# Routers on the plain activations, norms by a diagonal product, adaptive units moved between products

## The chip, the cores and the metric

The kernel runs on one core of a Trainium2 chip. The metric is the device time of one execution in microseconds; three executions of the kernel before took 1907.48, 1910.18 and 1911.77 us (median 1910.18). A profiled execution of it took 1905.38 us; its trace spans 1903.6 us. All rows below are of that execution.

## The reference, cut to what matters

`x` is 256 tokens of 1024 numbers. Two blocks follow each other; every layer has a norm in front and adds its output to `x`.

- First block: `x += token_mixer(rmsnorm(x, norm_mix))`, then `x += hierarchical_moe(rmsnorm(x, norm_ffn))` with 32 experts of width 512, of which each token takes two.
- Second block, layer 0: `x += g_m * attention(modulate(x, g, sh_m, sc_m))` (its keys also come from a context), then `x += g_f * ec_moe(modulate(x, g, sh_f, sc_f))` with 16 experts of width 1024, each of which takes its 32 best tokens. Layer 1: the same with a short convolution in place of the attention.

```python
def rmsnorm(x, g):
    return x * lax.rsqrt(jnp.mean(x * x, axis=-1, keepdims=True) + EPS) * g
def modulate(x, g, shift, scale):
    return rmsnorm(x, g) * (1 + scale) + shift
# sh_m, sc_m, g_m, sh_f, sc_f, g_f of a layer:
m = jax.nn.silu(cond) @ w_ada + b_ada          # 1024 x 6144, split in six
# router of the second block's experts:
aff = jax.nn.softmax(h @ w_router, axis=-1)    # h = modulate(x, ...)
```

The weights of all experts and projections are float32 and are read from HBM once, about 713 MB in all.

## The kernel before, in words

**Stages.** `build` (L1452) runs five stages one after the other: `mixer1` (L599), `moe1` (L977), `mixer2` (L1165, attention), `moe2(0)` (L1384), `mixer3` (L1330, convolution), `moe2(1)`. `x` lies in SBUF as [128, 2, 1024]: 128 tokens on the partitions, two halves `c`. After `moe1` stands a branch for overfull experts (`moe1_overflow`, L1050); no instruction is moved across it.

**The weight stream.** `Stream` (L170) issues all weight loads on SyncE's queue, in the order that `plan` (L395) lists them, each of 2 MB into a slot of a ring. The ring has 6 slots; three more ("rooms" X, Y, Z) are lent while no mixer needs them. A load is issued once the slot of its tile is free, that is once the last reader of the tile before has run; `done` is called in program order behind it. So the stream runs ahead of the compute by up to 9 slots and then stands.

**Norms.** `norm_T` (L275) makes the normed and transposed activations. For each `c`: ScalarE squares `x` in two halves with a running sum, VectorE adds the two sums and EPS, GpSimd takes the power -0.5 (`rstd`, L264), VectorE and ScalarE write `x * rstd` into `xh`, TensorE transposes it in eight 128x128 pieces into PSUM, and `evac_mod` applies gain and shift, piece by piece, in turn on ScalarE and VectorE. In a mixer the result is then split into a high and a low fp32r part (`split`, L309).

**Products of the mixers.** `staged` (L314) splits a 128x512 piece of the weights on ScalarE (`wh`) and VectorE (`wl`), three buffers deep; `three` (L323) runs the three fp32r products (high by high, low by high, high by low). `chain` (L154) runs the projections one after the other: product, then the rest of what follows the product before it (`finish`: head norms, rope, transposes). A projection holds two of the four PSUM banks `pj`. `flow` (L143) runs the heads of the attention as overlapping units.

**Adaptive units.** `ada_unit` (L530) makes one of the six vectors of a layer: 2 x 8 float32 matmuls of [128 x 32] by [128 x 512] on two weight tiles, an evacuation each, 8 transposes, a small reduction. (0,0), (0,1), (0,2) run inside the two flows of `mixer1`, (0,3) at its end (L844), (0,4) in front of the norm of `mixer2` (L1180), (0,5) and (1,0) among its heads, (1,1) and (1,2) at its end (L1326), (1,3) and (1,4) between the halves of `mixer3`, (1,5) at its end (L1380).

**Routers.** `moe1` and `moe2` norm and transpose `x` (`norm_T`, L983 and L1391), multiply by the router's weights (`router`, L847) and then find each expert's tokens on VectorE, with short products on TensorE between. `experts` (L875) gathers the tokens of four experts at a time from `xh` (L890, `xg_ps`), multiplies by gate and up (L904, `gu_ps`), after which the slots of these weights are free, transposes, multiplies by down (L931) and scatters into four PSUM banks `y` (L943). `add_out` (L972) adds them to `x`.

**Order.** The order on SyncE is the program's; on the other engines a planner orders the instructions by its own estimate of when their operands are there, in program order where two are ready.

Of the kernel before, what the change touches and what calls it, by code (L numbers as in the profile page):

```python
# [10 lines left out]
F32 = mybir.dt.float32  # L11
# [36 lines left out]
def small_inputs(I):  # L48
# [105 lines left out]
def chain(units):  # L154


    last = iter(())
    for product, finish in units:
        next(product, None)
        for _ in last:  # L160
            pass
        for _ in product:
            pass
        next(finish, None)
        last = finish
    for _ in last:
        pass

# [59 lines left out]
class Net:  # L228
    def __init__(self, ctx, tc, I, packs, out):
        self.packs = packs  # L230
        self.ctx, self.tc, self.nc, self.I, self.out = ctx, tc, tc.nc, I, out
        self.flip = 0

# [41 lines left out]
    def norm_T(self, src, xh, dst, G, SH, ps, tag, bufs, chunks=(0, 1)):  # L275


        nc = self.nc
        for c in chunks:
            ss = self.sm.tile([128, 2], F32, tag="nh_ss", name="nh_ss")  # L280
            x, t = src(c), xh(c).rearrange("p k m -> p (k m)")
            for h in range(2):
                nc.scalar.activation(t[:, h * 512:h * 512 + 512], x[:, h * 512:h * 512 + 512], AF.Square,
                                     scale=1.0 / 32, accum_out=ss[:, h:h + 1])
            r = self.rstd(ss[:, 0:1], [128, 1], ss[:, 1:2])
            v = x.rearrange("p (m k) -> p k m", k=8)
            for h in range(2):
                i, o = v[:, 4 * h:4 * h + 4, :], xh(c)[:, 4 * h:4 * h + 4, :]
                if h == 0:
                    nc.vector.tensor_scalar(o, i, r, None, op0=ALU.mult)  # L290
                else:
                    nc.scalar.activation(o, i, AF.Copy, scale=r)
            for kq in range(2):
                b = ps.tile([128, 4, 128], F32, tag=tag, name="xT_ps", bufs=bufs)
                for kk in range(4):
                    nc.tensor.transpose(b[:, kk, :], xh(c)[:, 4 * kq + kk, :], self.ident)
                if isinstance(dst, tuple):
                    for kk in range(4):
                        k = 4 * kq + kk
                        self.evac_mod(b[:, kk, :], b[:, kk, :], G[:, k:k + 1], None if SH is None else SH[:, k:k + 1])  # L300
# [3 lines left out]
                for kk in range(4):  # L304
                    k = 4 * kq + kk
                    self.evac_mod(dst(k)[:, c * 128:c * 128 + 128], b[:, kk, :], G[:, k:k + 1],
                                  None if SH is None else SH[:, k:k + 1])

    def split(self, hi, lo, src):  # L309

        self.nc.scalar.activation(hi, src, AF.Copy)  # L311
        self.nc.vector.tensor_tensor(lo, src, hi.bitcast(F32), op=ALU.subtract)  # L312

    def staged(self, src, wk):  # L314
# [5 lines left out]
        self.split(v[0], v[1], src)  # L320
# [55 lines left out]
    def rope_tables(self, rt, wk, cos, sin, gains, parts):  # L376
# [4 lines left out]
        for qk in range(2):  # L381
# [13 lines left out]
    def plan(self):  # L395
        I, add = self.I, self.st.add

        def ada(l, v):
            src = I["ada_w_2"][l].rearrange("(p k) f -> p k f", k=8)
            for hf in range(2):  # L400
# [33 lines left out]
        for c0 in (768, 0):  # L434
# [1064 lines left out]
```

## Time and profile before

| | us |
|---|---|
| median of three executions (lowest, highest) | 1910.18 (1907.48, 1911.77) |
| profiled execution | 1905.38 |
| span of its trace | 1903.6 |
| TensorE matmuls busy | 1327.5 (70%) |
| VectorE busy | 502.8 (26%) |
| ScalarE busy | 382.2 (20%) |
| GpSimd busy | 97.4 (5%) |

The profile's page cuts the span in 40 slices of 47.6 us and gives for each the bytes that the DMA engines moved. Its line GB/s reads about 430 in the slices of the experts, and between 127 and 373 in the first five, in the 15th to 19th and in the 28th to 31st, which are the mixers. Times of the trace count from the start of the span. "PE" is TensorE, "PEld" its weight loads, "DVE" VectorE, "ACT" ScalarE, "POOL" GpSimd, "SP" SyncE. A float32 matmul of the program shows as two instructions, a transpose as one.

### The profile page before, as it was taken

The page shows a single profiled execution, that of the slowest core. Times are in us where ns is not written, and L with a number is a line of the kernel's source. Part 1 is how long each engine was busy: PE and PEld are TensorE (multiplying, and loading weights), DVE is VectorE, ACT ScalarE, POOL GpSimd, SP SyncE. Part 2 cuts the span into 40 slices and gives each one's busy share as a digit, 9 for nine tenths or more (in the row PEclk, how much of TensorE's full clock was granted, in tenths as well). Part 3 has the DMA queues.
Part 4 walks back from the last instruction along what each step waited for, and adds up shares of the span by engine and source line. Part 5 has one row for each costly group of instructions (what it writes and reads, how often), then busy time and mean ns, then how long its engine had stood idle before and what let it go on. Part 6 is the DMA issues. An engine that isn't in the chain of part 4 may idle for free.

```text
span 1903.6 us, 27293 instructions
## 1 busy us (share of the span) xinstructions
PE 1327.5 (70%) x11779; PEld 734.0 (39%) x11779; DVE 502.8 (26%) x1256; ACT 382.2 (20%) x838; POOL 97.4 (5%) x151
## 2 busy tenths in 40 slices
PE   6989776676788678997656555565996664654744
PEld 4666443343444356463222221223983221211311
DVE  4566311121111056563010010103664110101101
ACT  6545100120101054651000000003443000000000
POOL 2120000000000024110000000000000000000000
PEclk9989988898999899898887787778997877877878
DMA  9746899999999994378999999999957999999998
GB/s 373 282 156 250 358 429 429 429 427 425 401 415 430 424 355 159 127 317 339 431 431 429 431 430 431 431 430 416 346 229 307 430 430 432 430 430 430 431 430 338
DMA packets 97690, 716.14 MB, mean 376 GB/s; under 512 B 5664, under 2 KB 7840, under 8 KB 56480
## 3 DMA queue, kind: packets, MB, share of 16 engines
q1 hardware_dynamic: 97104, 712.80, 89.8%
q8 instruction: 93, 1.52, 0.3%
q0 software_dynamic: 464, 1.57, 0.2%
q14 instruction: 29, 0.24, 0.0%
HBM read 713.30 MB, written 1.05 MB: 375 GB/s over the span
## 4 chain that ended last, share of the span: by engine, by line
DMA 44%; PE 24%; DVE 3%; ACT 2%; POOL 2%; issue 1%; SPq 0%; POOLq 0%; DVEq 0%; ACTq 0%
DMA w<-in_moe_w_up 17%; DMA w<-in_moe_w_gate 12%; DMA w<-in_moe_w_down 9%; PE gu_ps L904 7%; PE cv_ps L328 4%; DMA w<-in_w_up 3%; PE pj_ps L328 2%; DMA w<-in_conv_w_in 2%; PE cx_ps L1140 2%; PE d_ps L931 2%; PE ada_ps L540 1%; PE o_ps L328 1%; PE xg_ps L890 1%; DMA w<-in_attn_w_in 1%; POOL rs_r L272 1%
## 5 line engine op out<-in xcount | busy, mean ns | idle before, releaser
L904 PE MATMUL gu_ps<-w,xgT 128*32 128x256 f32 (+1 forms) x4096 | 434.9, 584 | 312.0 <-DMA w<-in_moe_w_up 258.5
L904 PEld LDWEIGHTS gu_ps<-w,xgT 128*32 128x32 f32 x4096 | 147.5, 129 | 576.0 <-issue 259.2
L910 DVE TENSOR_TENSOR h<-gu_ps,hs 64x256 f32<-64x256 f32 (+1 forms) x64 | 46.6, 728 | 783.1 <-ACT hs L909 783.1
L909 ACT ACTIVATE hs<-gu_ps 64x256 f32<-64x256 f32 (+1 forms) x64 | 31.2, 488 | 923.9 <-PE gu_ps L904 923.9
L931 PE MATMUL d_ps<-w,eh 128*32 128x256 f32 x3072 | 201.4, 410 | 21.7 <-DMA w<-in_moe_w_down 9.4
L311 ACT ACTIVATE wh<-w 128x512 fp32r<-128x512 f32 x184 | 115.1, 631 | 130.0 <-PE pj_ps L328 44.0
L312 DVE TENSOR_TENSOR wl<-w,wh 128x512 fp32r<-128x512 f32 x184 | 125.2, 689 | 60.5 <-ACT wh L311 57.1
L931 PEld LDWEIGHTS d_ps<-w,eh 128*32 128x32 f32 x3072 | 96.2, 117 | 103.8 <-issue 25.2
L328 PE MATMUL pj_ps<-wh,roomX 128*128 128x512 f32 x352 | 102.1, 404 | 6.7 <-DVE xn L355 3.4
L923 PE MATMUL t_ps<-kp,h 64*128 64x64 f32 x192 | 25.2, 238 | 88.6 <-DVE h L910 85.6
L272 POOL TENSOR_TENSOR rs_r<-rs_r,mhalf 128x1 f32<-128x1 f32 (+3 forms) x48 | 49.7, 1035 | 588.1 <-DVE rs_r L269 327.9
L328 PEld LDWEIGHTS pj_ps<-wh,roomX 128*128 128x128 f32 x352 | 65.8, 191 | 25.4 <-issue 7.1
L890 PE MATMUL xg_ps<-Sg,xh 128*128 128x128 f32 x512 | 70.6, 297 | 4.1 <-DVE Sg L883 3.5
L328 PE MATMUL cv_ps<-roomX,wh 128*128 128x256 f32 x384 | 70.2, 284 | 1.8 <-ACT roomX L311 1.5
L890 PEld LDWEIGHTS xg_ps<-Sg,xh 128*128 128x128 f32 x512 | 65.2, 207 | 14.2 <-issue 8.8
L328 PE MATMUL pj_ps<-wl,roomX 128*128 128x512 f32 x176 | 58.3, 407 | 13.2 <-DVE wl L312 13.2
L923 PEld LDWEIGHTS t_ps<-kp,h 64*128 64x128 f32 x192 | 16.6, 137 | 128.6 <-DVE h L910 114.1
L328 PEld LDWEIGHTS cv_ps<-roomX,wh 128*128 128x128 f32 x384 | 60.1, 192 | 3.9 <-ACT roomX L311 2.6
L328 PE MATMUL cv_ps<-roomX,wl 128*128 128x256 f32 x192 | 54.2, 283 | 0.0
L540 PE MATMUL ada_ps<-w,sc 128*32 128x512 f32 x384 | 48.1, 617 | 2.8 <-DVEq L1057 2.8
L943 PE MATMUL z<-ysb,WT 32*128 32x256 f32 x512 | 36.7, 400 | 16.5 <-DVE ysb L938 16.5
L1140 PE MATMUL cx_ps<-w,roomX 128*128 128x512 f32 x96 | 43.6, 602 | 0.0
(366 smaller groups left out, 1315.7 us busy)
## 6 DMA issues: line engine op xcount, KB each, us to landing
w<-in_moe_w_gate SPq DMA_DIRECT2D x64, 2048.0 KB, 38.7
w<-in_moe_w_up SPq DMA_DIRECT2D x64, 2048.0 KB, 29.0
w<-in_moe_w_down SPq DMA_DIRECT2D x63, 2048.0 KB, 33.0
w<-in_w_gate SPq DMA_DIRECT2D x32, 2048.0 KB, 20.1
w<-in_w_up SPq DMA_DIRECT2D x32, 2048.0 KB, 23.2
w<-in_w_down SPq DMA_DIRECT2D x32, 2048.0 KB, 22.0
w<-in_ada_w SPq DMA_DIRECT2D x24, 2048.0 KB, 12.2
w<-in_attn_w_in SPq DMA_DIRECT2D x7, 2048.0 KB, 14.3
```

Source lines behind the costliest of these rows:

```text
L272: nc.gpsimd.tensor_tensor(r, r, self.mhalf.to_broadcast(shape), op=ALU.pow)
L311: self.nc.scalar.activation(hi, src, AF.Copy)
L312: self.nc.vector.tensor_tensor(lo, src, hi.bitcast(F32), op=ALU.subtract)
L328: self.nc.tensor.matmul(o, l[a], r[b], start=first and n == 0, stop=last and n == 2)
L540: nc.tensor.matmul(b[32 * j:32 * j + 32, :], self.sc[:, 4 * kk + j, :], w[:, 4 * kk + j, :], start=kk == 0, stop=kk == 1)
L890: nc.tensor.matmul(b[:, k, :], self.xh[:, c, 2 * kq + k, :], Sg[:, c].rearrange("p e s -> p (e s)"), start=c == 0, stop=c == 1)
L904: nc.tensor.matmul(gu[32 * j:32 * j + 32, :], xgT[:, k, sl:sl + 32], w[:, n * Fh:n * Fh + Fh], start=k == 0, stop=k == 7)
L910: nc.vector.tensor_tensor(h, gu[0:64, :].rearrange("p (m c) -> p c m", c=nch), hs.rearrange("p (m c) -> p c m", c=nch), op=ALU.mult)
L923: nc.tensor.transpose(ht[:, c * 64:c * 64 + 64], h[:, c, :], self.ident[0:64, 0:64])
L931: nc.tensor.matmul(d[32 * j:32 * j + 32, :], hT[:, c, n * 32:n * 32 + 32], wd(n, c, j), start=i == 0, stop=i == 2 * nch - 1)
L943: nc.tensor.matmul(y[j][:, c, :], WT[r, c * 128:c * 128 + 128], ysb[r, :], start=e == 0 and c == 0, stop=e == ne - 1, skip_group_check=True)
L1140: nc.tensor.matmul(b, xr["hT"][:, k, c * 128:c * 128 + 128], w[:, k, :], start=k == 0, stop=k == 7)
```

## The change

- The norm of a mixer no longer writes `x * rstd`. ScalarE squares `x` in one piece, GpSimd adds EPS and takes the power, VectorE writes `diag(rstd)`, and TensorE multiplies the eight pieces of `x` by it, which transposes and scales at once. In `mixer1` the gain moves into the staging of the weights.
- `held` keeps an instruction in program order on its engine. It is put on the squares, on the first four stagings behind a norm, and on a few small ones.
- The routers' norm: the mixers' last additions to `x` are followed by squares on ScalarE (`squares`), the routers transpose `x` itself (`raw_T`), the gain is multiplied into the router's weights beforehand, the shift becomes a bias of the logits (`router_bias`), and `rstd` scales the logits. The gather reads `x` with `rstd` in the selection matrix `Sg`. The residual `x` is added into the PSUM banks by eight products with the identity at expert 3, and `new_x` copies the banks out.
- Adaptive units: (0,0) and (0,1) go between the first three products of `mixer1`, (0,2) between the two of its second chain, (0,3) into the router of `moe1`, (0,4) behind the norm of `mixer2`, (1,0) and (1,1) between its five products, (1,2) among its heads, (0,5) and (1,5) into the routers of `moe2`. The order of their loads follows. The rows of the gate of `mixer3` are made at expert 2 of `moe2(0)`.
- The silu of the conditions and its data come first in `mixer1`; the forget gate comes behind two steps of the first product.

```diff
-def chain(units):
+def chain(units, fill=iter(()), last=iter(())):
...
         next(finish, None)
+        next(fill, None)
         last = finish
...
     def rstd(self, ms, shape, more=None):
-        if more is None:
-            nc.vector.tensor_scalar(r, ms, EPS, None, op0=ALU.add)
...
+            nc.gpsimd.tensor_tensor(r, ms, more, op=ALU.add)
+        nc.gpsimd.tensor_scalar(r, ms, EPS, None, op0=ALU.add)
         nc.gpsimd.tensor_tensor(r, r, self.mhalf.to_broadcast(shape), op=ALU.pow)
...
+            self.held(nc.scalar.activation(junk(c), x, AF.Square, scale=1.0 / 32, accum_out=ss))
+            r = self.rstd(ss, [128, 1])
+            nc.vector.tensor_scalar(self.diag[:, c, :], self.ident, r, None, op0=ALU.mult)
...
-                    nc.tensor.transpose(b[:, kk, :], xh(c)[:, 4 * kq + kk, :], self.ident)
+                    nc.tensor.matmul(b[:, kk, :], v[:, 4 * kq + kk, :], dg, start=True, stop=True)
...
+    def staged(self, src, wk, g=None):
...
+        if self.late:
+            self.late -= 1
+            for ins in both:
+                self.held(ins)
...
     def add_gated(self, b, gate, c, hf):
...
+        self.squares(b, c, hf)
+    def squares(self, b, c, hf):
+        self.nc.scalar.activation(b, self.x[:, c, hf * 512:hf * 512 + 512], AF.Square, scale=1.0 / 32,
+                                  accum_out=self.ss[:, hf, c:c + 1])
...
+    def raw_T(self, hT, ps):
+        v = self.x.rearrange("p c (m k) -> p c k m", k=8)
+        for kq in range(2):
+            for c in range(2):
+                b = ps.tile([128, 4, 128], F32, tag="a", name="xT_ps", bufs=3)
+                for kk in range(4):
+                    self.nc.tensor.transpose(b[:, kk, :], v[:, c, 4 * kq + kk, :], self.ident)
+                self.evac(hT[kq][:, :, c * 128:c * 128 + 128], b, c == 0)
...
             self.evac(r, b, True)
             self.st.done(("ada", l, v, hf))
-        for _ in range(1 + wait):
+            yield
+        for _ in range(wait):
             yield
...
+    def experts(self, ne, F, posm, comb, rk, G, SH, tiles, wk, ps, y, hook=None, gate=None, first=None):
...
+                nc.vector.tensor_tensor(Sg, Sg, rk[:, :, None, None].to_broadcast([128, 2, 4, 32]), op=ALU.mult)
...
-                            nc.tensor.matmul(b[:, k, :], self.xh[:, c, 2 * kq + k, :],
+                            nc.tensor.matmul(b[:, k, :], xv[:, c, 2 * kq + k, :],
...
+            if e == 0:
+                first()
...
+            if e == 3:
+                for c in range(2):
+                    for j in range(4):
+                        nc.tensor.matmul(y[j][:, c, :], self.ident, self.x[:, c, 256 * j:256 * j + 256], start=False,
+                                         stop=False, skip_group_check=True)
...
-    def add_out(self, y):
-        for j in range(4):
-            xs = self.x[:, :, 256 * j:256 * j + 256]
-            self.nc.vector.tensor_tensor(xs, y[j], xs, op=ALU.add)
+    def new_x(self, y):
+        for c in range(2):
+            for j in range(4):
+                self.evac(self.x[:, c, 256 * j:256 * j + 256], y[j][:, c, :], j % 2 and not c)
...
     def moe2(self, l):
...
-            self.norm_T(lambda c: self.x[:, c, :], lambda c: self.xh[:, c], hT, G, SH, ps, "a", 3)
-            z = self.router(wk, ps, hT, f"wr2{l}")[:, :, 0:16]
+            r = self.rstd(self.ss[:, 0, :], [128, 2], self.ss[:, 1, :])
+            self.raw_T(hT, ps)
+            z = self.router(wk, ps, hT, f"wr2{l}")
...
+            for c in range(2):
+                nc.vector.scalar_tensor_tensor(aff[:, c, :], z[:, c, 0:16], r[:, c:c + 1], self.rbias, op0=ALU.mult, op1=ALU.add)
...
+            fill = self.ada_unit(l, 5, wk, ps, "a", "a", 3, 0, 3, row)
+            next(fill)
...
             for c in range(2):
                 nc.tensor.transpose(b[:, c, :], aff[:, c, :], self.ident)
+            next(fill)
...
     def mixer2(self):
...
-            self.ada(0, 4, wk, ps, "pj", "tp", 4, 0, 2, q2[:, 2048:3072])
...
+            self.ada(0, 4, wk, ps, "pj", "tp", 4, 0, 2, q2[:, 2048:3072])
...
-                   pair(1792, 0, 0, 0, lambda c: v[:, c, 256:768])])
+                   pair(1792, 0, 0, 0, lambda c: v[:, c, 256:768])],
+                  merged(*(self.ada_unit(1, i, wk, ps, "pj", "tp", 4, 0, 2, q2[:, 2048:3072]) for i in range(2))))
...
-            for i, (l, v_) in ((4, (0, 5)), (9, (1, 0))):
-                units.insert(i, self.ada_unit(l, v_, wk, ps, "pj", "tp", 4, 0, 2, row))
+            units.insert(4, self.ada_unit(1, 2, wk, ps, "pj", "tp", 4, 0, 2, row))
...
-            flow([self.ada_unit(1, 1 + i, wk, ps, "pj", "tp", 4, 0, 2, q2[:, 1024 * i:1024 * i + 1024])
-                  for i in range(2)])
...
     def mixer3(self):
...
-            self.gate_rows(1, 2, gate, row, ps, "tp")
...
+            self.router_bias(1, ps, "tp", 2)
...
-            for _ in self.ada_unit(1, 5, wk, ps, "pj", "tp", 5, 0, 2, row):
-                pass
```

## Rows read from the trace of the kernel before

**Rows 1.** Windows by stage: us, busy of each engine, granted clock, DMA share, GB/s.

```profile
0.00:177.00 177.00, 150.67 (x817) 109.22 (x818) 104.63 (x287) 94.60 (x212) 33.49 (x48) 0.96 0.68 255
177.00:208.00 31.00, 21.21 (x199) 13.68 (x197) 15.69 (x64) 11.04 (x24) 2.75 (x9) 0.89 0.80 336
208.00:667.00 459.00, 338.47 (x3992) 186.31 (x3992) 71.06 (x209) 50.93 (x134) 12.72 (x18) 0.91 1.00 422
667.00:846.00 179.00, 153.89 (x748) 102.32 (x744) 110.44 (x248) 96.98 (x218) 41.77 (x50) 0.95 0.60 228
846.00:884.00 38.00, 29.28 (x223) 15.42 (x216) 18.58 (x63) 14.29 (x29) 1.10 (x2) 0.87 0.76 315
884.00:1314.00 430.00, 250.16 (x2432) 98.83 (x2432) 42.63 (x90) 21.14 (x44) 0.26 (x4) 0.80 1.01 430
1428.00:1468.00 40.00, 26.94 (x183) 14.92 (x182) 18.48 (x59) 14.05 (x27) 1.10 (x2) 0.74 0.68 284
```

**Rows 2.** Timeline from mixer1's last product to moe1's first expert: start, us, instruction.

```profile
177.32 3.64 PE L540 MATMUL ada_ps<-w,sc 128*32 128x512 f32 x32
...
184.40 1.53 PE L296 MATMUL xT_ps<-kp,xh 128*128 128x128 f32 x12 [0.28 <-DVE mod L552]
...
188.62 0.35 DVE L260 TENSOR_SCALAR hTh<-xT_ps,kp 128x128 f32<-128x128 f32 x1 [0.44 <-ACT hTh L255]
...
192.40 0.17 DVE L987 TENSOR_TENSOR zg<-rt_ps,kp 128x8 f32<-128x8 f32 x1 [2.30 <-PE rt_ps L865]
...
198.85 5.75 PE L890 MATMUL xg_ps<-Sg,xh 128*128 128x128 f32 x32 [1.39 <-DVE Sg L883]
...
204.53 3.66 PE L904 MATMUL gu_ps<-w,xgT 128*32 128x256 f32 x64
```

**Rows 3.** Timeline from mixer2's last product to moe2(0)'s first expert.

```profile
845.82 7.07 PE L540 MATMUL ada_ps<-w,sc 128*32 128x512 f32 x64
...
860.60 0.41 DVE L262 TENSOR_SCALAR hTh<-xT_ps,G,SH 128x128 f32<-128x128 f32 x1 [0.53 <-ACT hTh L257]
...
862.88 0.19 DVE L1395 TENSOR_REDUCE ec_m<-rt_ps 128x2 f32<-128x32 f32 x1 [0.72 <-PE rt_ps L865]
...
876.92 7.07 PE L904 MATMUL gu_ps<-w,xgT 128*32 128x512 f32 x64
```

**Rows 4.** Timeline from mixer3's last product to its router's logits.

```profile
1428.06 3.64 PE L540 MATMUL ada_ps<-w,sc 128*32 128x512 f32 x32
...
1446.52 0.19 DVE L1395 TENSOR_REDUCE ec_m<-rt_ps 128x2 f32<-128x32 f32 x1 [0.72 <-PE rt_ps L865]
```

**Rows 5.** Windows of the mixers' chains of products, columns as in rows 1.

```profile
30.00:60.00 30.00, 26.60 (x126) 20.70 (x125) 17.77 (x34) 16.85 (x29) 9.61 (x12) 1.00 0.77 293
125.00:140.00 15.00, 9.52 (x38) 6.31 (x36) 9.95 (x26) 5.01 (x14) 4.36 (x4) 0.82 0.54 199
705.00:757.00 52.00, 42.72 (x188) 31.69 (x187) 35.27 (x75) 20.19 (x40) 26.12 (x29) 1.00 0.39 138
```

**Rows 6.** Timeline: first product of mixer1, of mixer2, transposes ahead of mixer3's.

```profile
17.15 0.74 PE L328 MATMUL pj_ps<-wh,roomX 128*128 128x512 f32 x2 [2.35 <-DVE roomX L312]
...
685.54 0.72 PE L328 MATMUL pj_ps<-wh,roomX 128*128 128x512 f32 x2 [0.62 <-DVE roomX L312]
...
1319.43 3.43 PE L296 MATMUL xT_ps<-kp,xh 128*128 128x128 f32 x16 [5.65 <-DVE rs_r L271]
```

**Rows 7.** Timeline of mixer2: three of the four reads of its first product's banks.

```profile
697.52 0.58 ACT L346 ACTIVATE ro<-pj_ps 128x512 f32<-128x512 f32 x1
...
701.28 0.69 DVE L355 TENSOR_TENSOR xn<-pj_ps,rs_r 128x512 f32<-128x512 f32 x1 [1.54 <-POOL rs_r L272]
...
708.05 0.69 DVE L355 TENSOR_TENSOR xn<-pj_ps,rs_r 128x512 f32<-128x512 f32 x1 [1.54 <-POOL rs_r L272]
```

**Rows 8.** One line's instructions (ns: least, median, most), and GpSimd's groups.

```profile
L269 DVE TENSOR_SCALAR rs_r<-hss x20: 158/164/171, 37.1 to 749.8; 128x8 f32<-128x8 f32 x14, 128x4 f32<-128x4 f32 x6
...
L683 POOL TENSOR_SCALAR ext<-cum 128x8 f32<-128x8 f32 x4 | 0.8, 202 | 0.0
```

More of the change, by code (lines that the diff above doesn't have):

```diff
@@ L167, in chain, with merged, row_of @@
         pass
+def merged(a, b):
+    next(a)
+    yield
+    next(a)
+    yield
+    next(a, None)
+    next(b)
+    yield
+    next(b)
+    yield
+    next(b, None)
+    yield
+def row_of(*units):
+    for u in units:
+        yield from u
 class Stream:
@@ L486, in setup @@
         self.mod = {}
+        self.diag = cp.tile([128, 2, 128], F32, name="diag")
+        self.ss = cp.tile([128, 2, 2], F32, name="ss")
         self.cnt16 = cp.tile([128, 2, 128], BF16, name="cnt16")
@@ L670, in product @@
                 w = st.take(("in1", col))
-                yield from self.product(lambda k: w[:, k, :], self.columns(hT), 8, b, wk, every)
+                yield from self.product(lambda k: w[:, k, :], self.columns(hT), 8, b, wk, every, gm)
                 st.done(("in1", col))
@@ L1045, in hook @@
                     steps.pop(0)()
-            self.experts(32, 512, posm, comb, self.P("g_ffn"), None, tiles, wk, ps, y, hook)
-            self.add_out(y)
+                if e == 5:
+                    for c in range(2):
+                        nc.vector.tensor_scalar(self.xh[:, c], self.x[:, c].rearrange("p (m k) -> p k m", k=8), rk[:, c:c + 1],
+                                                None, op0=ALU.mult)
+            rk = sm.tile([128, 2], F32, name="rk", bufs=1)
+            nc.vector.tensor_copy(rk, r)
+            self.experts(32, 512, posm, comb, rk, self.P("g_ffn"), None, tiles, wk, ps, y, hook, None, lambda: next(fill, None))
+            self.new_x(y)
     def moe1_overflow(self):
@@ L1403, in moe2 @@
                 nc.tensor.transpose(b[:, c, :], aff[:, c, :], self.ident)
+            next(fill)
             aT = wk.tile([16, 256], F32, tag="WT", name="affT")
@@ L1446, in tiles, with first, hook @@
                 return halves("g"), halves("u"), (lambda n, c, j: wd[n][:, c, j * 256:j * 256 + 256]), done
-            gate = self.gate_quarters(l, 5, wk.tile([128, 256], F32, name="gate", bufs=1), wk, ps, "a", 3)
-            self.experts(16, 1024, posm, aff, G, SH, tiles, wk, ps, y, None, gate)
-            self.add_out(y)
+            gate = wk.tile([128, 256], F32, name="gate", bufs=1)
+            def first():
+                next(fill, None)
+                self.gate_quarters(l, 5, gate, wk, ps, "a", 3)
+            def hook(e):
+                if (l, e) == (0, 2):
+                    self.gate_rows(1, 2, gated, row, ps, "a", 3)
+            self.experts(16, 1024, posm, aff, rk, G, SH, tiles, wk, ps, y, hook, gate, first)
+            self.new_x(y)
     def build(self):
```

243 lines of the change are left out of this document (141 added, 102 removed).

## The prediction

> **What bounds the kernel now.** First I read the windows by stage, for two columns only: the DMA share and the GB/s. In the experts' stages the DMA engines are full (share 1.00 and 1.01, 422 and 430 GB/s) [rows 1]: their length is bytes by rate, and TensorE, busy 338 of 459 and 250 of 430 us there, has room. In the mixers they are not: from 0 to 177 the share is 0.68 at 255 GB/s, from 667 to 846 0.60 at 228, and in the stretches from a mixer's last product to the first expert 0.80, 0.76 and 0.68 [rows 1]. There TensorE is busy 151 of 177 and 154 of 179 us [rows 1]: the stream stands because the ring is full of weights that no product has used yet. The ring empties when the first expert's gate and up products run (204.53, 876.92) [rows 2, 3]. So a microsecond taken off before that moment moves everything behind it by one, as long as the stream has idle time left there: 31 x 0.20 = 6.2 us, 38 x 0.24 = 9.1 and 40 x 0.32 = 12.8 in the three stretches alone [rows 1], and 0.32 x 177 = 57 and 0.40 x 179 = 72 in the mixers before the first two. Work added inside an expert stage costs nothing until it uses up the difference above.
>
> Then I read the timeline of the three hand-overs, because each shows work in front of the router: after the last product TensorE makes adaptive units (3.64, 7.07 and 3.64 us) [rows 2 to 4] before transposes and router. Last the windows of the chains of products, for TensorE's gaps: 3.4 of 30, 5.5 of 15 and 9.3 of 52 us idle [rows 5].
>
> **Prices.** A transpose 1.53/12 = 0.13 us [rows 2], and 3.43/16 = 0.21 after TensorE had been idle [rows 6]; an fp32 128x128 product 5.75/16 = 0.36 [rows 2]; a unit 3.64 [rows 2] plus 8 transposes, 1.0, so 4.7, a half 1.8; a 128x512 read of PSUM on VectorE 0.69 [rows 7]; a 128x128 piece with gain 0.35 to 0.41 [rows 2, 3]. A norm by products with diag(rstd) is 16 x 0.36 = 5.8 us of TensorE in place of 16 x 0.13 = 2.0, +3.7 in each of three mixers; it saves a pass over `x` (0.69).
>
> **The parts, in order of time.**
>
> 1. *Start of mixer1.* First product at 17.15, after a wait for the split activations [rows 6]. The 16 pieces with gain go (16 x 0.35 on two engines, 2.8), the pass (0.7), and the forget gate steps behind two steps of the product; +3.7 for the products. At best the last two columns of that are hidden, -6; at worst the products cost 1.6 times as much, as the transposes did after idle time, +2. I take -2.5. The loads that move (constants to ScalarE's queue, the rest of them further back on SyncE's) are hidden by that same wait, as long as x is what comes last.
>
> 2. *Units between mixer1's products.* Three halves and a set of transposes (6.5) enter the first chain, two halves (3.6) the second; both leave the flows, where TensorE had other work. The gaps that they could fill are 3.4 and 5.5 [rows 5], so -8 at best. Against it stands a wait that is new: a half takes one of the four `pj` banks, so the next product's second bank is the first bank of the product before. In mixer2 that bank is first read at 697.52 and given up at 701.28 + 0.69 = 701.97 [rows 7]: 4.5 us, of which the half covers 1.8 and the next product's first column block, three buffers deep (9 matmuls of 42.72/188 = 0.23, 2.1 us) [rows 5], most of the rest. I put 1 us on each of the two places of the first chain. In the second both banks are taken at once; its wait is long, 3 us. On SyncE's queue the third product's tile comes behind the unit's two, fifth in line: five of 2.1 MB at 293 GB/s [rows 5] are 36 us, and its product is due at about 14.6 + 2 x 48 x 0.23 + 3.6 = 40: in time, with little to spare. Sum -2, ends -8 and +8.
>
> 3. *Unit (0,3) and router of moe1.* Before: 177.32 to the last piece at 188.62, then 3.8 us to the logits at 192.40 [rows 2]. After: additions 2 x 0.69 = 1.4, 16 transposes 2.0, a last evacuation 0.7, from 177.3 to 181.4, then the same 3.4 to 3.8 gives 184.8 to 185.2: -7.4. A second pass over `Sg` +0.4. The unit's two halves (3.6) stand in VectorE's search between the logits (192.40) and the gather (198.85) [rows 2], 6.5 us; if that cover is gone they come back whole. I take -7, ends -3 and -9.
>
> 4. *Start of mixer2.* First product at 685.54 [rows 6]. Unit (0,4) leaves the front, -4.7; the products add 3.7, half of it beside the pieces' gains. -2.5, ends -4.7 and +3.7.
>
> 5. *Units between mixer2's products.* Four halves and two sets of transposes, 9.5 us, into 52 us with 9.3 idle [rows 5]. VectorE is busy 35.3 of these 52 and GpSimd 26.1 [rows 5]; the gaps are waits inside products, which a half in front of a product only partly takes. I let 7.5 of the 9.5 be absorbed, and add 4 places x 1 us for the bank: +6, ends 0 and +13.
>
> 6. *Heads.* Two units among them become one: 4.7 less, some of it in gaps, -4, ends 0 and -4.7.
>
> 7. *Units (1,1), (1,2) and router of moe2(0).* Before: 845.82, 7.07 us of units, last piece at 860.60, logits at 862.88 [rows 3]. After: 4 x 0.69 of gated additions, 2.0 and 0.7, then the same 862.88 - 860.60 - 0.41 = 1.9: 845.8 + 2.8 + 2.7 + 1.9 = 853.2, that is -9.7; small operations on the logits +0.6. Unit (0,5) now comes in two halves beside VectorE's search, which lasts until the first expert at 876.92. -9, ends -5 and -10.
>
> 8. *Start of mixer3.* The products cost 3.7 more, behind 5.65 us of idle TensorE [rows 6]; no unit leaves. +1, ends -1 and +5.
>
> 9. *Unit (1,5) and router of moe2(1).* 1428.06 to 1446.52 is 18.5 us [rows 4], against 7.4 to 9 by the sum of step 7: -9.5 with the small operations, ends -5 and -11.
>
> 10. *The rest.* The routers' bias, folded gains, and gate rows moved: +1, ends 0 and +3. Inside the experts (identity products 8 x 0.72 = 5.8 at one expert, unit ends, copies of `x`) nothing, for the stream hides it [rows 1].
>
> Sum: -2.5 - 2 - 7 - 2.5 + 6 - 4 - 9 + 1 - 9.5 + 1 = -28.5. The profiled execution took 1905.4, which gives 1876.9; the three executions lie 2.1 to 6.4 above it, the median 4.8. I predict 1880.0.
>
> *A rule against it.* The EPS addition moves from VectorE to GpSimd in all 48 `rstd`. VectorE's takes 0.16 us, a small GpSimd operation of the same shape 0.20 [rows 8], so +0.04 each, and a hand-over between the two engines falls away: nothing in my sum. The Trainium skill (GPSIMD Engine Reference, section 4.1, Engine selection) says that elementwise additions belong on VectorE, since GpSimd is about twice as slow on operations with two inputs and about even with one. By the twice-as-slow figure it would be 48 x 0.16 = +7.7 us, if every one stood on the path, and the time 1888; the row has 0.20 against 0.16, on an operation with one input, and bears that figure out only in part.
>
> **Rivals.**
>
> - *Only the routers gain.* The chains are bound by the products' followers, not by TensorE, so each inserted half is added whole; the starts gain nothing. Steps 3, 7, 8, 9, 10 stay (-23.5), 5 is +9.5, 2 is +4, 6 is -2: -12, about 1897. For it: TensorE's gaps sit inside products. Against: VectorE has 17 of 52 us free [rows 5].
> - *The gaps are filled.* Step 1 -4, 2 -8, 4 -4, 5 +1, 6 -4.7, routers -25.5: -45, about 1864. For it: the gaps add up to 18 us [rows 5].
> - *The wait for the bank is the whole product's.* If a product behind a half waits until both banks of the one before are read, at 708.05 + 0.69 = 708.74, then each place costs 708.74 - 697.52 - 1.8 = 9.4 us [rows 7]. At seven places (two and one in mixer1, four in mixer2) that is 7 x 8.4 = 59 more than I counted: about 1939. It makes the kernel slower from 28.5/7 = 4.1 us per place above my 1. For it: four banks and five holders. Against: the two column blocks wait for one bank each.
> - *GpSimd's addition* as above: 1888.
> - *It does not do what it says*: the stream has no idle time to give, and the routers' 25 us come back as a wait for weights; about 1908. Against it stand shares of 0.68 to 0.80 [rows 1].
>
> **Chances.** Forecast 0.53, with its own range of 1866 to 1892; gaps filled 0.13; only the routers 0.15; GpSimd 0.05; bank 0.10; no effect 0.04. About 0.2% (3.8 us) is what a measurement of this kernel can tell from no change. Faster 0.85, same 0.04, slower 0.11. The range 1856 to 1901 leaves out the bank case and the tails.
>
> **What would show it.** Last product of a mixer to logits: about 8, 8 and 9 us in place of 15, 17 and 18. First product of mixer1 before 15 us, of mixer2 at about the same distance from moe1's end less 2.5. In the chains, idle TensorE ahead of a product's second column block below 2 us: right; waits of 4 us and more there, ended by the reads of `pj`: the bank rival. The experts' stages at 422 to 430 GB/s: right; below 415, work that I held for hidden is not. The prediction is wrong if the chains grow by more than 15 us in all, or the mixers' shares of DMA do not rise.

## The result: slower, and where the time went

The changed kernel takes 1925.31 us (median of four runs, 1923.21 to 1929.25) against 1909.14: ratio 1.0086, 95% interval 1.0065 to 1.0107. I had forecast 1880 and a chance of 0.11 for slower. Its profiled execution took 1923.21 us with a span of 1921.5, 17.9 more than before.

The ends of the stages come from the timeline of TensorE. First the rows of the kernel before that did not stand above: last scatter of each experts' stage, and the starts behind it.

```profile
666.53 1.15 PE L943 MATMUL y<-ysb,WT 32*128 32x256 f32 x16 [0.55 <-DVE ysb L248]
...
1312.63 1.15 PE L943 MATMUL z<-ysb,WT 32*128 32x256 f32 x16 [0.55 <-DVE ysb L938]
...
1326.08 0.39 PE L328 MATMUL cv_ps<-roomX,wh 128*128 128x256 f32 x1 [1.51 <-ACT roomX L311]
...
1461.05 7.07 PE L904 MATMUL gu_ps<-w,xgT 128*32 128x512 f32 x64
...
1895.77 1.15 PE L943 MATMUL z<-ysb,WT 32*128 32x256 f32 x16 [0.55 <-DVE ysb L938]
```

The same places in the changed kernel: first product, last product and first gate product of each hand-over, last scatter.

```profile
17.89 1.21 PE L361 MATMUL pj_ps<-wh,roomX 128*128 128x512 f32 x4
...
173.92 0.61 PE L361 MATMUL pj_ps<-wl,oTd 128*128 128x512 f32 x2
...
201.07 3.66 PE L989 MATMUL gu_ps<-w,xgT 128*32 128x256 f32 x64
...
674.65 1.15 PE L1030 MATMUL y<-ysb,WT 32*128 32x256 f32 x16 [0.55 <-DVE ysb L271]
...
697.89 1.17 PE L361 MATMUL pj_ps<-wh,roomX 128*128 128x512 f32 x4
...
858.27 0.63 PE L361 MATMUL pj_ps<-wl,high 128*128 128x512 f32 x2
...
885.05 7.07 PE L989 MATMUL gu_ps<-w,xgT 128*32 128x512 f32 x64
...
1325.03 1.15 PE L1030 MATMUL z<-ysb,WT 32*128 32x256 f32 x16 [0.55 <-DVE ysb L1025]
...
1342.31 0.58 PE L361 MATMUL cv_ps<-roomX,wh 128*128 128x256 f32 x1 [4.14 <-ACT wh L335]
...
1446.30 0.63 PE L361 MATMUL o_ps<-wl,zTh 128*128 128x512 f32 x2
...
1473.47 7.07 PE L989 MATMUL gu_ps<-w,xgT 128*32 128x512 f32 x64
...
1913.88 1.15 PE L1030 MATMUL z<-ysb,WT 32*128 32x256 f32 x16 [0.56 <-DVE ysb L1025]
```

Subtracting them (an end is start plus duration) gives this table, with the other ends from [rows 2 to 4, 6]:

| stretch | before | after | difference | my step |
|---|---|---|---|---|
| start to last product of mixer1 | 177.3 | 174.5 | -2.8 | 1, 2: -4.5 |
| to first expert of moe1 | 27.2 | 26.5 | -0.7 | 3: -7 |
| experts of moe1 | 463.2 | 474.7 | **+11.6** | 0 |
| to first product of mixer2 | 17.9 | 22.1 | +4.2 | 4: -2.5 |
| products and heads of mixer2 | 160.3 | 161.0 | +0.7 | 5, 6: +2 |
| to first expert of moe2(0) | 31.1 | 26.2 | -4.9 | 7: -9 |
| experts of moe2(0) | 436.9 | 441.1 | **+4.3** | 0 |
| to first product of mixer3 | 12.3 | 16.1 | +3.8 | 8: +1 |
| products of mixer3 | 102.0 | 104.6 | +2.6 | 10: +1 |
| to first expert of moe2(1) | 33.0 | 26.5 | -6.5 | 9: -9.5 |
| experts of moe2(1) | 435.9 | 441.6 | **+5.7** | 0 |

The mixers and hand-overs together gained 3.6 us instead of 28.5; the experts, which I had put at nothing, lost 21.6. So about 46 us lie between my sum and the measurement, 24.9 of them in the mixers and hand-overs and 21.6 in the experts; the second part made the kernel slower. Two views show what is different there. The windows of the changed kernel that answer to [rows 1] (us, busy of each engine, granted clock, DMA share, GB/s), and one steady stretch of each kernel inside the second block's experts, here the changed kernel's:

```profile
208.00:667.00 459.00, 361.82 (x3932) 216.13 (x3936) 69.11 (x203) 46.55 (x124) 14.31 (x24) 0.94 0.99 413
884.00:1314.00 430.00, 265.90 (x2429) 114.77 (x2432) 45.52 (x96) 23.62 (x46) 2.17 (x4) 0.82 0.99 421
900.00:1300.00 400.00, 247.07 (x2282) 107.61 (x2274) 40.49 (x85) 20.27 (x41) 0.13 (x2) 0.82 1.01 427
```

```profile
900.00:1300.00 400.00, 227.00 (x2162) 89.44 (x2164) 38.66 (x82) 19.04 (x40) 0.13 (x2) 0.78 1.01 430
```

The second fence is the kernel before. The DMA engines are as full (1.01), yet move 427 GB/s in place of 430. That is no stall: each byte takes longer. And TensorE and its weight loads are busier, mostly because of one group. Groups by line, before and then after (busy us, mean ns of one):

```profile
L890 PE MATMUL xg_ps<-Sg,xh 128*128 128x128 f32 x512 | 70.6, 297 | 4.1 <-DVE Sg L883 3.5
L890 PEld LDWEIGHTS xg_ps<-Sg,xh 128*128 128x128 f32 x512 | 65.2, 207 | 14.2 <-issue 8.8 <-DVE Sg L883 3.5 <-ACT xgT L257 0.9
```

```profile
L975 PE MATMUL xg_ps<-Sg,x 128*128 128x128 f32 x512 | 128.0, 411 | 0.1
L975 PEld LDWEIGHTS xg_ps<-Sg,x 128*128 128x128 f32 x512 | 124.1, 335 | 7.7 <-issue 7.7
```

The gather's stationary operand is now `x` with every eighth column, and its load takes 335 ns instead of 207. A gather takes 7.9 us instead of the 5.75 of [rows 2]:

```profile
193.26 7.88 PE L975 MATMUL xg_ps<-Sg,x 128*128 128x128 f32 x32
```

### The profile page after: what moved, and what is told of

Read it like the earlier page. It is cut to its first block, busy times and chain, and to the rows that moved or that the text cites. A ratio compares the mean times of both kernels' runs of the same rounds, so it can differ in the third digit from the quotient of the medians.

```text
span 1921.5 us, 27516 instructions
## 1 busy us (share of the span) xinstructions
PE 1402.9 (73%) x11927; PEld 817.8 (43%) x11927; DVE 496.7 (26%) x1213; ACT 361.0 (19%) x786; POOL 110.6 (6%) x200
## 4 chain that ended last, share of the span: by engine, by line
DMA 36%; PE 19%; DVE 3%; ACT 1%; POOL 1%; issue 1%; SPq 0%; DVEq 0%; POOLq 0%; ACTq 0%
DMA w<-in_moe_w_up 21%; DMA w<-in_moe_w_gate 12%; PE gu_ps L989 6%; PE cv_ps L361 4%; DMA w<-in_moe_w_down 3%; PE pj_ps L361 2%; PE d_ps L1018 2%; PE xg_ps L975 1%; PE o_ps L361 1%; PE ada_ps L574 1%; PE sc_ps L1327 0%; PE av_ps L1348 0%; PE xT_ps L318 0%; POOL rs_r L299 0%; DVE nm L1330 0%
## 5 line engine op out<-in xcount | busy, mean ns | idle before, releaser
L989 PE MATMUL gu_ps<-w,xgT 128*32 128x256 f32 (+1 forms) x4096 | 417.2, 564 | 268.6 <-DMA w<-in_moe_w_up 236.3
L989 PEld LDWEIGHTS gu_ps<-w,xgT 128*32 128x32 f32 x4096 | 141.4, 125 | 521.2 <-DMA w<-in_moe_w_up 243.9
L1018 PE MATMUL d_ps<-w,eh 128*32 128x256 f32 x3072 | 208.1, 421 | 21.6 <-DMA w<-in_moe_w_down 10.2
L996 ACT ACTIVATE hs<-gu_ps 64x256 f32<-64x256 f32 (+1 forms) x64 | 31.1, 487 | 866.8 <-PE gu_ps L989 866.8
L975 PE MATMUL xg_ps<-Sg,x 128*128 128x128 f32 x512 | 128.0, 411 | 0.1
L975 PEld LDWEIGHTS xg_ps<-Sg,x 128*128 128x128 f32 x512 | 124.1, 335 | 7.7 <-issue 7.7
L336 DVE TENSOR_TENSOR wl<-w,wh 128x512 fp32r<-128x512 f32 x136 | 92.4, 693 | 45.6 <-ACT wh L335 40.5
L335 ACT ACTIVATE wh<-w 128x512 fp32r<-128x512 f32 x136 | 85.0, 631 | 100.3 <-PE cv_ps L361 36.9
L574 PE MATMUL ada_ps<-w,sc 128*32 128x512 f32 x384 | 52.0, 598 | 0.3 <-DVE roomX L336 0.3
L1030 PE MATMUL z<-ysb,WT 32*128 32x256 f32 x512 | 36.7, 400 | 16.3 <-DVE ysb L1025 16.3
L1005 PE MATMUL t_ps<-kp,wdup 128*128 128x128 f32 x128 | 30.8, 322 | 21.9 <-DVE eh L271 9.9
L1025 DVE TENSOR_TENSOR ysb<-d_ps,gate 128x256 f32<-128x256 f32 x32 | 13.6, 424 | 125.1 <-PE d_ps L1018 125.1
## 6 DMA issues: line engine op xcount, KB each, us to landing
w<-in_ada_w SPq DMA_DIRECT2D x24, 2048.0 KB, 15.1
```

Source lines behind the costliest of these rows:

```text
L335: return (self.nc.scalar.activation(hi, src, AF.Copy), self.nc.vector.tensor_tensor(lo, src, hi.bitcast(F32), op=ALU.subtract))
L574: nc.tensor.matmul(b[32 * j:32 * j + 32, :], self.sc[:, 4 * kk + j, :], w[:, 4 * kk + j, :], start=kk == 0, stop=kk == 1)
L975: nc.tensor.matmul(b[:, k, :], xv[:, c, 2 * kq + k, :], Sg[:, c].rearrange("p e s -> p (e s)"), start=c == 0, stop=c == 1)
L989: nc.tensor.matmul(gu[32 * j:32 * j + 32, :], xgT[:, k, sl:sl + 32], w[:, n * Fh:n * Fh + Fh], start=k == 0, stop=k == 7)
L996: nc.scalar.activation(hs, gu[64:128, :], AF.Silu)
L1005: nc.tensor.transpose(wt[:, c * 128:c * 128 + 128], wdup, self.ident)
```

## Experiments

Two theories for the experts. *Slot theory*: the new tiles `diag` and `ss` (and others) moved the ring of weight slots in SBUF from a multiple of 512 bytes to 288 bytes behind one, and writing there is slower. (These offsets follow from the sizes of the tiles allocated in front; no view shows an address.) *Gather theory*: the strided weight loads cost the time, and perhaps the rate. A third, the queue that ScalarE now uses for the constants, falls with the first two runs.

**The slots.** The shift alone, put into the kernel before (`e2_shift288`):

```diff
+        pad = cp.tile([128, 72], F32, name="pad")
+        nc.gpsimd.memset(pad, 0.0)
         self.cnt16 = cp.tile([128, 2, 128], BF16, name="cnt16")
```

> The kernel before with 288 bytes more in front of the ring, nothing else. Slot theory: the experts' stages of the second block lose 1.1% and the first block's about 5 us: 1909 + 14 = 1923. Gather and queue theories: 1909.

Measured 1925.51 us, ratio 1.0079 (1.0060 to 1.0097): the shift by itself costs as much as the whole change. Its three experts' stages take 469.2, 440.8 and 441.9 us, together 16 more than before. The other way round, the changed kernel with its ring brought back (`e1_pad512`):

```diff
         self.ss = cp.tile([128, 2, 2], F32, name="ss")
+        pad = cp.tile([128, 56], F32, name="pad")
+        nc.gpsimd.memset(pad, 0.0)
...
-                    ow = sm.tile([128, 2, 32], F32, name="ov_w")
+                    ow = sm.tile([128, 2, 32], F32, name="ov_w", bufs=1)
```

> The changed kernel with 224 bytes put in front of the weight ring (and one buffer of an unused branch halved), so that its slots begin at multiples of 512 bytes, as before the change; in the changed kernel they begin 288 bytes behind one. Slot theory: the weights' writes run at 430 GB/s again in the second block's experts (changed kernel 421 and 419 over the same kind of window), each of these stages about 436 us from first gate product to last scatter instead of 441, the first block's experts 5 us shorter, in all about 1911 us. Gather theory (the strided reads of x by TensorE cost the rate) and queue theory (constants on ScalarE's queue): rate and time as in the changed kernel, 1925.

Measured 1912.63 us, 1.0015 (1.0004 to 1.0025), and the queue on ScalarE is still in it. The experts' stages take 470.2, 437.0 and 436.0 us, together 14 less than in the changed kernel. Two more pads ask how coarse the boundary is: 8 floats (`e1_pad64`, ring 320 bytes behind a multiple of 512; there `ow` keeps its buffers) and 120 floats (`e1_pad256`, 256 bytes behind one).

> The same with 32 bytes, so that the slots begin at multiples of 64 bytes but 320 behind a multiple of 512. If a coarse boundary (512) decides the rate: as the changed kernel, 421 GB/s and 1925 us. If 64 bytes are enough: 430 GB/s and 1911 us. Gather and queue theories: 1925.

> The changed kernel with its ring 256 bytes behind a multiple of 512. If 512 is the boundary: between 1912.6 (offset 0) and 1921 (offset 320), rate below 428 GB/s. If a smaller power of two is enough: 1912.6 and 430 GB/s.

Measured 1921.03 (1.0066, 1.0046 to 1.0085) and 1910.48 us (1.0010, 0.9999 to 1.0022). The steady stretch in the four kernels, in the order `e2_shift288`, `e1_pad64`, `e1_pad256`, `e1_pad512`:

```profile
900.00:1300.00 400.00, 232.49 (x2266) 91.91 (x2258) 39.10 (x83) 19.15 (x40) 0.13 (x2) 0.79 1.01 427
```

```profile
900.00:1300.00 400.00, 246.92 (x2282) 107.19 (x2274) 40.52 (x85) 20.26 (x41) 0.13 (x2) 0.82 1.01 427
```

```profile
900.00:1300.00 400.00, 243.24 (x2220) 104.93 (x2216) 40.08 (x84) 20.26 (x41) 0.13 (x2) 0.81 1.01 430
```

```profile
900.00:1300.00 400.00, 249.22 (x2298) 107.41 (x2290) 40.53 (x85) 20.31 (x41) 0.13 (x2) 0.82 1.01 430
```

427 GB/s at 288 and 320, 430 at 0 and 256, whatever TensorE does beside it. So 256 bytes are enough, 64 are not (my guess of 512 was too coarse). A pad moves every tile that is allocated behind it; that it is the ring which matters is read from the rate of the weights. The two rates as rounded account for about 9 of the 14 to 16 us; where the rest goes is not shown. The Trainium skill (DMA: Bandwidth & Descriptors, section How a descriptor splits into AXI transactions) has transfers cut at 256-byte boundaries, with spent beats where a descriptor starts off one; it gives this for reads, the runs show the loss where the destination in SBUF is off the boundary.

**The gather.** `e3_gather` keeps the ring at 288 and lets each product of the gather read 128 neighbouring columns, which takes the columns in another order than the experts' weights expect.

```diff
-        xv = self.x.rearrange("p c (m k) -> p c k m", k=8)
+        xv = self.x.rearrange("p c (k m) -> p c k m", k=8)
```

> The changed kernel with the gather reading 128 neighbouring columns of x in each product instead of every eighth: the columns stand in another order, so the experts' output is not the reference's. Strided-weights theory: a gather of 32 instructions takes 5.8 us instead of 7.9, the three hand-overs save 2.1 us each, and the first block's experts get back the 4 us for which the stream stood at 477 to 570 us: 1925 - 10 = 1915, the rate in the second block unchanged at 420. If the strided reads also cost the weights' rate: 430 GB/s and 1901. Slot theory alone: 1925.

Measured 1912.83 us, 1.0025 (1.0009 to 1.0040). The mean weight load is back at 207 ns, the steady rate stays at 426 to 427: the stride costs TensorE's time, not the weights' rate.

```profile
L975 PEld LDWEIGHTS xg_ps<-Sg,x 128*128 128x128 f32 x512 | 65.2, 207 | 9.6 <-issue 7.3
```

About half of what it costs lies in the experts of moe1, where two context projections and two gathers fall together: from 489 to 501 us TensorE is busy 12.00 of 12 us, where it was busy 10.64 before. The stretch 477 to 573 us, before, after and `e3_gather`:

```profile
477.00:573.00 96.00, 76.78 (x867) 42.41 (x867) 15.71 (x46) 10.94 (x30) 4.38 (x5) 0.93 0.99 409
```

```profile
477.00:573.00 96.00, 77.47 (x750) 46.37 (x750) 14.40 (x40) 9.88 (x27) 5.81 (x8) 0.93 0.94 383
```

```profile
477.00:573.00 96.00, 77.36 (x882) 42.65 (x886) 15.37 (x44) 10.95 (x30) 4.58 (x7) 0.94 0.99 407
```

The share falls from 0.99 to 0.94: here the stream does stand, 96 x 0.05 = 5 us, and what it loses in a stage that it bounds does not come back. moe1's experts take 468.7 us in `e3_gather` instead of 474.7; the three hand-overs save 2.0, 1.5 and 2.1.

**Both repaired.** `f1_xh` pads the ring and lets the gather read a copy again; `f2_pool` makes the copy on GpSimd.

```diff
-                nc.vector.tensor_tensor(Sg, Sg, rk[:, :, None, None].to_broadcast([128, 2, 4, 32]), op=ALU.mult)
...
-                            nc.tensor.matmul(b[:, k, :], xv[:, c, 2 * kq + k, :],
+                            nc.tensor.matmul(b[:, k, :], self.xh[:, c, 2 * kq + k, :],
...
+    def normed_x(self, r):
+        for c in range(2):
+            v = self.x[:, c].rearrange("p (m k) -> p k m", k=8)
+            if c:
+                self.nc.vector.tensor_scalar(self.xh[:, c], v, r[:, c:c + 1], None, op0=ALU.mult)
+            else:
+                self.nc.scalar.activation(self.xh[:, c], v, AF.Copy, scale=r[:, c:c + 1])
```

> The changed kernel with the ring at multiples of 512 bytes and the gather on a copy: beside the router ScalarE and VectorE write x * rstd, piece by piece next to each other, into xh as the kernel before did, the gather reads it, and rstd no longer multiplies Sg; the units of the routers use another buffer and the gate rows of the convolution mixer are made in it again. Slot and strided-weights theories together: -13 and -12.5, another -1.5 for the second pass over Sg at three hand-overs: 1925 - 27 = 1898, 430 GB/s, gather 5.8 us. If the two overlap, or the copy stands in the router's way: 1905 to 1912.

Measured 1902.75 us, 0.9959 (0.9944 to 0.9974): faster than before, 5 short of the sum. Its twelve executions spread from 1896.0 to 1911.2, and the profiled one took 1906.7, so its windows show an execution 4 us longer than the median. The miss is in the first hand-over: the window from the last product to the first expert, `f1_xh`:

```profile
174.70:205.30 30.60, 24.25 (x127) 13.82 (x127) 12.63 (x50) 7.49 (x15) 1.14 (x3) 0.61 0.82 335
```

TensorE's granted clock is 0.61 there. ScalarE's copy (2.16 us) stood in front of the router's evacuations, and TensorE waited 0.88 us for them in the middle of the transposes. It stayed at 1.2 GHz, the lower of its two levels, until 193: the unit's matmuls, 3.63 us in the changed kernel, took 6.22.

```profile
178.10 2.16 ACT L921 ACTIVATE xh<-x,rs_r 128x1024 f32<-128x1024 f32 x1 [1.43 <-POOL rs_r L299]
...
189.24 6.22 PE L576 MATMUL ada_ps<-w,sc 128*32 128x512 f32 x30
```

> The kernel with the copy of x * rstd, made by GpSimd instead of ScalarE and VectorE. If the copy stood in the router's way (ScalarE's 2.2 us in front of the evacuations, TensorE then at a granted clock of 0.61 from the last product of the first mixer to the first expert): that stretch falls from 30.6 to about 24.5 us, the next from 26.7 to 24.5, in all 1903 - 7 = 1896. If the low clock there has another cause: no change, 1903. If GpSimd is too slow for the gather: 1905 to 1910.

Measured 1896.87 us, 0.9934 (0.9916 to 0.9952). The first window is now 23.7 us at a clock of 0.86:

```profile
175.60:199.30 23.70, 17.18 (x126) 11.48 (x125) 11.56 (x49) 5.56 (x14) 8.86 (x5) 0.86 0.98 412
```

In both kernels the clock had fallen before the evacuations: TensorE was idle for 2.03 us behind the last product, and in the transposes that follow the granted clock goes to 0.50. With the copy on GpSimd it comes back early, with the copy on ScalarE and VectorE it does not; `f2_pool` (two windows), then `f1_xh`:

```profile
179.00:181.00 2.00, 2.00 (x11) 1.74 (x9) 0.69 (x1) 0.87 (x2) 1.91 (x1) 0.50 0.96 410
183.00:185.00 2.00, 1.81 (x21) 1.08 (x22) 0.13 (x1) 0.38 (x1) 2.00 (x1) 1.00 1.00 426
```

```profile
183.00:185.00 2.00, 1.46 (x17) 0.60 (x16) 0.42 (x1) 0.00 (x0) 0.00 (x0) 0.50 1.11 471
```

The other profiled kernels agree: this window is 30.5 us in `f3_oldnorm` and `h_nofill`, which have the copy on ScalarE and VectorE, and 24.3 in `g1_best` and `g2_mix`, which have it on GpSimd. Which of the two halves decides, ScalarE's or VectorE's, is not shown.

**The units between products.** `h_nofill` is `f1_xh` with units (1,0) and (1,1) behind the five products (and their loads too).

```diff
-                  merged(*(self.ada_unit(1, i, wk, ps, "pj", "tp", 4, 0, 2, q2[:, 2048:3072]) for i in range(2))))
+            for _ in merged(*(self.ada_unit(1, i, wk, ps, "pj", "tp", 4, 0, 2, q2[:, 2048:3072]) for i in range(2))):
+                pass
```

> The kernel with the copy, but units (1,0) and (1,1) behind the five products of the attention mixer in place of between them. If the halves between the products fill gaps, this adds most of their 9.5 us: 1904 to 1907. My step's sum (6 of 9.5 kept): +3.5, 1901.5. If halves between products are added whole or delay the product by the bank: no change or faster, 1890 to 1898.

Measured 1908.76 us, 0.9982 (0.9968 to 0.9997), 0.23% over `f1_xh` beside it; the two intervals still overlap. Products and heads take 163.2 us instead of 161.1, so the place is worth 2 us there in the two profiled executions; the rest came in the last stages (104.9 for the third mixer, 438.3 for the last experts) and is not settled. As far as this shows it, step 5 had the sign right.

**The norm by products.** `f3_oldnorm` is `f1_xh` with the mixers' norm as it was (and without holding the first stagings).

```diff
-            self.held(nc.scalar.activation(junk(c), x, AF.Square, scale=1.0 / 32, accum_out=ss))
...
-                    nc.tensor.matmul(b[:, kk, :], v[:, 4 * kq + kk, :], dg, start=True, stop=True)
+                    nc.tensor.transpose(b[:, kk, :], xh[:, 4 * kq + kk, :], self.ident)
```

> The same with the norm of the mixers as the kernel before had it (x * rstd written, then transposed). If the products with diag(rstd) cost what the trace shows (16 products in 7.9 us, strided), the starts of the second and third mixer are each 2 to 4 us shorter (22.1 and 16.1 us from the last scatter to the first product with products, 17.9 and 12.3 before): 1898 - 6 = 1892. If the gain in starts is from elsewhere (order, the held instructions, the branch): no change, 1898.

Measured 1905.60 us, 0.9964 (0.9950 to 0.9979): no difference to `f1_xh`. By stage there is one. The third mixer starts after 12.1 us instead of 16.3, the first after 15.1 instead of 18.1, but the first mixer's rest then takes 160.5 instead of 156.6. In the second mixer the branch (below) hides the difference: there the old norm starts after 21.3 us with a short branch, the products after 18.4 with one as short (`k_more`), so in that place the products are the better ones by 3 us. In the third mixer of the changed kernel the 16 products took 7.87 us, 0.49 each, as their stationary operand is the strided `x` too (the granted clock is 0.50 from 1330 to 1334 and 0.96 from there to 1338.2, and their pace is the same), and TensorE then waited 4.14 us:

```profile
1330.30 7.87 PE L318 MATMUL xT_ps<-diag,x 128*128 128x128 f32 x32 [4.12 <-DVE diag L312]
...
1343.49 0.63 PE L361 MATMUL cv_ps<-roomX,wh 128*128 128x256 f32 x2
```

A pair of the convolution's products takes 0.63 us at the lower clock, 0.40 at the higher, which it reaches at 1348: 2 us of "products of mixer3, +2.6".

**The branch.** In front of the second mixer ScalarE waited 5.24 us for TensorE's branch at the overflow test. That one instruction (duration in ns), before and after:

```profile
L1057 PEldq COMPARE_BRANCH  x1: 367/367/367, 667.2 to 667.2; - x1
```

```profile
L1164 PEldq COMPARE_BRANCH  x1: 6246/6246/6246, 675.3 to 675.3; - x1
...
681.75 1.06 ACT L310 ACTIVATE xh<-x 128x1024 f32<-128x1024 f32 x1 [5.24 <-PEq L1164]
```

`k_more` is `e1_pad512` with more instructions on TensorE far ahead of it:

```diff
+                if e == 2:
+                    b = ps.tile([128, 64], F32, tag="a", name="more", bufs=3)
+                    for _ in range(64):
+                        nc.tensor.matmul(b[:, 0:32], self.cnt16[:, 0], self.cnt16[:, 1, 0:32], start=True, stop=True)
```

> The changed kernel with its ring at multiples of 512 bytes and 64 more small bf16 matmuls (2 us) inside the third expert of the first block, where TensorE has room; they write what nobody reads. TensorE's branch behind that block took 6.2 us in the changed kernel and 0.37 before. If it hangs on where the branch lies in TensorE's instructions: some other value, 0.4 us if lucky, and then 3.5 us less before the attention mixer, 1909. If it hangs on what runs around it: 5.9 us again, 1912.6.

Measured 1907.01 us, 0.9985 (0.9973 to 0.9996):

```profile
L1170 PEldq COMPARE_BRANCH  x1: 352/352/352, 669.7 to 669.7; - x1
```

The start of the second mixer falls from 21.8 to 18.4 us. In `f3_oldnorm` and `g1_best`, whose old norm also changes how many instructions TensorE has in front of the branch, it takes 0.37 us; in all other kernels made from the changed one without the 64 matmuls 5.9 to 6.3. So the branch's price goes with where it lies in TensorE's instructions, which any edit can move. The Trainium skill (Runtime: NRT & Kernel Launch, section Instruction fetch mechanics) says that a taken branch whose target is not among the pages already loaded waits for their fetch; the runs fit that, though no view shows the fetch itself, and the branch took 6 us at a DMA share of 1.04.

**Better versions.** `g1_best` is `f2_pool` with the old norm in all mixers and unit (0,4) in front again; `g2_mix` is `f2_pool` with the old norm in the third mixer alone and the 64 matmuls of `k_more`.

> The kernel before it with two parts of the change undone in the mixers: x * rstd written and transposed in place of the products with diag(rstd), and unit (0,4) in front of the attention mixer's norm again. If these cost what the traces show (first scatter to first product 17.9 us with unit (0,4) in front, 21.3 with it behind; the third mixer's start 12.1 in place of 16.3): 1896 - 8 = 1888. If the planner gives the time back inside the mixers, as it did in the first one: 1894 to 1898.

> The kernel with the copy on GpSimd; in the convolution mixer alone x * rstd is written and transposed and its first stagings are not held, and 64 small matmuls shift TensorE's instructions in front of the branch. Branch by place in the instructions: 0.35 us and -3.4 us before the attention mixer. Norm of the third mixer: first scatter to first product 12.1 in place of 16.4, -4.3. Together 1896.9 - 7.7 = 1889. If the two gains are chance or are given back in the mixers: 1893 to 1897.

Measured 1892.34 (0.9907, 0.9889 to 0.9925) and 1890.27 us (0.9899, 0.9882 to 0.9915). In `g1_best` part of the gain went again: the second mixer starts after 19.3 us, but its products and heads take 165.8 instead of 161.2; why is not settled. In `g2_mix` both gains came: 18.4 and 12.1 us.

## Why the prediction was wrong, step by step

- **The step that failed**, and that turned the sign, is the last sentence of step 10: "Inside the experts ... nothing, for the stream hides it". It measured +21.6 us. It treated the stream's rate as given and looked only at TensorE's work. I never asked where the ring would lie once two tiles are added in front of it: -13 to -15 us when it is put right, +16 in the kernel before. And I listed the work inside the experts without the change of the gather's operand, though the diff has it.
- **The gather** stood in no term of the sum. The diff turns contiguous `xh` into `x` at a stride of eight; the rows had a price for contiguous pieces only, and I used it for both without bounding it. It cost about 2 us in each of three hand-overs and 6 in moe1.
- **Steps 3, 7 and 9**: the units' removal gave what I worked out up to the logits, nearly: the routers' logits came 4.5, 8.2 and 9.2 us earlier behind the last product, where I had 7.4, 9.1 and 9.5. The logits in the changed kernel:

```profile
185.12 0.42 DVE L1082 SCALAR_TENSOR_TENSOR ze<-rt_ps,rs_r,kp 128x36 f32<-128x36 f32 x2 [3.26 <-PE rt_ps L948]
...
867.79 0.38 DVE L1505 SCALAR_TENSOR_TENSOR aff<-rt_ps,rs_r,rbias 128x16 f32<-128x16 f32 x2 [0.72 <-PE rt_ps L948]
...
1456.23 0.38 DVE L1505 SCALAR_TENSOR_TENSOR aff<-rt_ps,rs_r,rbias 128x16 f32<-128x16 f32 x2 [0.72 <-PE rt_ps L948]
```

  The transposes waited for the squares on ScalarE (0.8 us each time) and read the strided `x`, at 0.16 to 0.22 us instead of 0.13, part of them at the lower clock (granted 0.65 from 176.5 to 179). Then the gather took back 2.1, and in moe1 the unit was not hidden whole: its evacuation stands in front of the router's exponential on ScalarE.

```profile
186.99 0.60 ACT L269 ACTIVATE xh<-ada_ps 128x512 f32<-128x512 f32 x1 [3.55 <-PE ada_ps L574]
187.48 0.20 ACT L1093 ACTIVATE ze<-ze 128x8 f32<-128x8 f32 x1
187.71 0.16 DVE L1095 TENSOR_REDUCE pg<-ze 128x2 f32<-128x8 f32 x1 [0.71 <-ACT ze L1093]
```

- **Steps 4 and 8**: mis-sized, +4.2 and +3.8 against -2.5 and +1. A product with diag(rstd) costs 0.49 us, not 0.36; in the second mixer the long branch cost 3.4 us (`e1_pad512` against `k_more`), which no row of before could show as a risk (0.37 us there).
- **Step 1** had the sign wrong, and luck hid it. The first product came at 17.89 us, 0.7 later than before, where I had it 2.5 earlier and had named 15 us as the sign of being right; in `f3_oldnorm`, with the old norm, it came at 15.1. The rest of the first mixer gained 3.5 where step 2 had 2, and so the two together read -2.8 against -4.5.
- **Steps 5 and 6** held: +0.7 against +2. The new wait for the bank was filled as I said, by the first column block of the next product: behind the half at 710.16 products follow without idle time, in an order of their own (two, one, three, one).

```profile
710.16 1.92 PE L574 MATMUL ada_ps<-w,sc 128*32 128x512 f32 x14
712.01 0.74 PE L361 MATMUL pj_ps<-wh,roomX 128*128 128x512 f32 x2
712.59 0.40 PE L361 MATMUL pj_ps<-wl,roomX 128*128 128x512 f32 x1
712.83 0.86 PE L361 MATMUL pj_ps<-wh,roomX 128*128 128x512 f32 x3
```

- **The rivals**: the slower one that I had named, the bank, did not happen. Nor did GpSimd's addition: it took 0.24 us (median, 128x8) where the row had 0.20, but addition and power together fell from 2.3 us (37.08 to 39.34 in the kernel before) to 2.0 (38.31 to 40.33). The sign came from a cause that no rival held; the signs that I had named did catch it in moe1, whose window fell to 413 GB/s, below my 415. With the two repairs (`f2_pool`, which takes the in-place gather out of the change) it is worth -0.66%, 13.5 us: the direction is right for what the forecast reasoned about, the size of 28.5 was still twice too large.

## What to carry to other kernels

Where a stage is bound by its DMA, ask of a change not only what it adds to the engines but where it moves the transfers' destinations: keep the ring of tiles at a multiple of 256 bytes. Before an operand is read in place to save a copy, price its stride on the engine that reads it; an engine with nothing else to do (here GpSimd, 7.7 us for both halves) can make the copy. And a stage's DMA share near 1.00 hides added work only on average: a gather that falls into a crowded stretch costs the stream time that it cannot get back.

## What the runs showed of the hardware

- Weights written into SBUF at 288 or 320 bytes behind a multiple of 512 ran at 427 GB/s, at 0 and 256 at 430; in the whole kernel the shift by 288 made 13 to 16 us.
- A 128x128 fp32 stationary operand with every eighth element took 335 ns to load, a contiguous one 207 on the mean. The strided gather took 7.9 us in each of three hand-overs, though the granted clock within it went from 0.50 to 1.00.
- The same branch took 0.35 to 0.37 or 5.9 to 6.3 us on TensorE; 64 small matmuls far in front of it took it from 5.88 to 0.35.
- In the first hand-over TensorE's granted clock was 0.61 with a copy on ScalarE and VectorE and 0.86 with the same copy on GpSimd: 30.6 against 23.7 us for the same products.
